# Levels and tokens of the RWKV blocks made for a whole block at a time, and the keyed products moved to earlier slots

## The chip, the cores and the metric

The kernel runs on one core of a Trainium2 chip. The metric is the device time of one execution in microseconds. A core has several engines with an instruction queue each: TensorE (PE: matmul, with its weight loads shown as PEld), VectorE (DVE), ScalarE (ACT), GpSimd (POOL) and SyncE (SP, which issues most DMAs).

## What is computed

The reference is a backbone of two layers over 512 latent and 256 context tokens of width 1024. In each layer one input projection feeds a convolution module and a two-way RWKV-7 recurrence side by side; an output projection and a SwiGLU FFN follow. The part that matters here is the recurrence, over tokens, for 8 heads of 64 and in both directions:

```python
def step(s, inp):
    r_t, k_t, v_t, w_t, kk_t, b_t = inp
    sa = -jnp.einsum("bhvk,bhk->bhv", s, kk_t)
    s = (s * w_t[:, :, None, :] + sa[..., None] * b_t[:, :, None, :]
         + v_t[..., None] * k_t[:, :, None, :])
    y = jnp.einsum("bhvk,bhk->bhv", s, r_t) if emit else None
    return s, y
```

The rest of a layer, cut to what surrounds it:

```python
ux = modulate(rmsnorm(x, norm1_g[l]), sh1, sc1) @ w_in[l]
yc, s_f, s_b = rwkv_scans(prep_c, s_zero, s_zero, emit=not last)
yx, _, _ = rwkv_scans(prep_x, s_f, s_b, emit=True)
mix_x = concatenate([conformer_conv(ux[..., :CONV_IN], *cv), rwkv_out(yx, prep_x, *post)])
x = x + gt1 * (mix_x @ w_out[l])
x = x + gt2 * swiglu(modulate(rmsnorm(x, norm2_g[l]), sh2, sc2), ffn_wg[l], ffn_wu[l], ffn_wd[l])
```

## The kernel before, in words

Per layer there is an input stage, a **mixer stage** and an FFN stage. Dense products (helper `mm`, L234) take their operands as a high and a low part in a fast f32 format (`wh`, `wl`, and `h` or `mid`); the small products of the recurrence are plain f32.

The mixer handles the recurrence in 12 **blocks** b per layer: pair p of heads (b // 3) and group gi of four chunks of 64 tokens (b % 3). Each block goes through these parts, all of them Python generators that yield between steps:

- `prep(b)`: for each direction two products with the low-rank weights `lr` on PE, then a chain of ScalarE and VectorE (tanh, a scan, exponentials, products) that leaves the keys `bk` and the keyed rows `KR`. Its temporaries `tmp` and `tw`, and `bk`, have one buffer each, `KR` has three.
- `z_part(b)`: `grams(b)` makes the keyed products `G` from `KR` and `bk` (two steps, half a block each), then `base(b)` sends their diagonal pieces out by DMA (`d0`), reads them back as `Dt`, inverts 64 pieces of 16x16 at once on VectorE (`XT`) and writes them to `dimg` in DRAM.
- `t_part(b, hf)`: `inverses` loads the small inverses `Tm` from `dimg`, and `levels` joins them to 64x64 inverses in four steps. In each, small products on PE (64x64 or 32x32) are evicted by ScalarE (`W`, `Tm`) or VectorE, and the next step uses them. At the end `KR` is copied into `G`. This is done for half a block (hf) at a time.
- `tokens(b, hf)`: transposes of `bk` into `tT` and of the values into `UV`, in two steps, also for half a block.
- `chain(b, s)`: the serial part, three steps for each of the four chunks.

The order is laid down by `weave`. In every block b all parts that are due (chains of b, levels and tokens of later blocks, prep and z_part of b + 2, convolution steps, the dense input projection cut into pieces) are lanes; a lane with `(first, slots)` and n steps puts step i at the slot first + slots * (i + 1) / n of 16, and the steps are issued in the order of their slots. PE keeps this order as it is written (`manual_schedule`); for the other engines and for SP's queue the framework's scheduler sets it. So an early slot means an early place in PE's queue, and PE waits there for what the step needs. The numbers stand in `PLAN`, per layer; `prologue` does the same for the first blocks of a layer.

Before the change the levels of a block's first half stand at slots 13 to 16 of the block ahead (`t0`), those of its second half at slots 1 to 4 of the block itself (`t1`); tokens are split in the same manner (`tok0`, `tok1`); prep(b + 2) has its steps at 3.3, 4.7 and 6, and z_part(b + 2) its steps at 10.3, 11.7 and 13.

Of the kernel before, what the change touches and what calls it, by code (L numbers as in the profile page):

```python
# [27 lines left out]
C = 64  # L28
# [52 lines left out]
def _pack(i):  # L81
# [45 lines left out]
    for nf in FPARTS:  # L127
# [22 lines left out]
         lanes={"chains": (0, 16), "t1": (0, 4), "t0": (12, 4), "tok1": (0.6, 3.26), "tok0": (13, 2), "prep": (2, 4),  # L150
                "z": (9, 4), "bonus": (3.89, 12.11), "pair_prep": (8, 8), "pair_out": (0, 13)},
         prologue={"pair_prep": (-1.3, 1.2), "prep0": (-0.3, 0.8), "z0": (0.9, 0.58), "tok00": (1.99, 1.08), "tok01": (1.94, 0.38), "prep1": (2.4, 1.0),
                "z1": (3.58, 0.6), "t0": (3.89, 0.86), "tok10": (4.12, 0.2)},
# [4 lines left out]
         lanes={"chains": (0, 16), "t1": (0, 4), "t0": (12.5, 3.5), "tok1": (0, 2.35), "tok0": (13, 2), "prep": (2, 4),  # L158
                "z": (9, 5.03), "bonus": (1.41, 13.65), "pair_prep": (7.33, 7.84), "pair_out": (0, 13)},
         prologue={"pair_prep": (-1.7, 1.2), "prep0": (-0.44, 0.74), "z0": (0.93, 0.52), "tok00": (1.52, 0.47), "tok01": (1.79, 0.39), "prep1": (1.97, 0.98),  # L160
                "z1": (3.6, 0.6), "t0": (3.98, 0.73), "tok10": (4.3, 0.3)},
# [9 lines left out]
def net(ctx: ExitStack, tc: tile.TileContext, I, out):  # L171
# [369 lines left out]
    for l in range(DEPTH):  # L541
# [213 lines left out]
        def prep(b):  # L755
# [42 lines left out]
            BS[b] = dict(KR=KR, bk=bk, vr=vr, pc=pc, emit=emit, G={}, tT={}, UV={}, T={})  # L798
# [35 lines left out]
        def tokens(b, hf):  # L834

            p, gi = divmod(b, 3)
            P, B = PS[p], BS[b]
# [3 lines left out]
            B["tT"][hf] = tT  # L841
            B["UV"][hf] = UV
            pt = [bank(), bank()]
            for s in range(2):
                for d in range(2):
                    cc = 2 * hf + s
                    o = 64 * (2 * s + d)
                    for hh in range(2):
                        hs = slice(64 * hh, 64 * hh + 64)
                        PE.transpose(pt[hh][:, o:o + 64],  # L850
                                     bk[hs, d, cc, hh:hh + 2, :].rearrange("p j t -> p (j t)"), ident[hs, hs])
            for hh in range(2):
                act(tT[:, hh, :, :], pt[hh][:, 0:256].rearrange("p (q j) -> p q j", j=64))
            yield
            pv = bank()
            for s in range(2):
                for d in range(2):
                    cc = 2 * hf + s
                    c0 = C * nat(0, gi, cc)
                    src = B["vr"][:, cc, :] if d else u[f"v{p}"][:, c0:c0 + 64]  # L860
                    o = 128 * (2 * s + d)
                    PE.transpose(pv[0:64, o:o + 128], src, ident)  # L862
            for hh in range(2):
                act(UV[64 * hh:64 * hh + 64, :, hh, :],
                    pv[0:64].rearrange("p (q h j) -> p q h j", q=4, h=2)[:, :, hh, :])
            yield
# [29 lines left out]
        def inverses(b, hf):  # L896

            Tm = s2.tile([128, 4, 2, 64], F32, tag="Tm", name=nm("Tm"), bufs=4)
            for hh in range(2):
                w = 64 - 64 * hh  # L900
                nc.sync.dma_start(out=Tm[w:w + 64].rearrange("p q x c -> p q (x c)"),
                                  in_=dimg[b % 3][8 * hf + 4 * hh:8 * hf + 4 * hh + 4, 0:8192]
                                  .rearrange("q (r c) -> r q c", c=128))
            BS[b]["T"][hf] = Tm

        def levels(b, hf):

            B = BS[b]
            Gt, Tm = B["G"][hf], B["T"][hf]
            lm = lmask.rearrange("p (x t) -> p x t", x=2)  # L910
            pW = bank()
            for q in range(4):
                for hh in range(2):
                    w = slice(64 - 64 * hh, 128 - 64 * hh)
                    mm(pW[w, 64 * q:64 * q + 64], Gt[w, hh, q, 0:64], Tm[w, q, 0, :])
            W = s2.tile([128, 4, 64], F32, tag="W", name=nm("W"))
            act(W.rearrange("p q t -> p (q t)"), pW[:, 0:256])
            yield
            pX = bank()
            for q in range(4):  # L920
                for hh in range(2):
                    w = slice(64 - 64 * hh, 128 - 64 * hh)
                    mm(pX[w, 64 * q:64 * q + 64], W[w, q, :], Tm[w, q, 1, :])
            for q in range(4):
                for hh in range(2):
                    w = slice(64 - 64 * hh, 96 - 64 * hh)
                    mm(pX[w, 256 + 32 * q:288 + 32 * q], Tm[w, q, 1, 0:32], W[w, q, 0:32])
            for hh in range(2):
                w = slice(64 - 64 * hh, 96 - 64 * hh)
                V.copy_predicated(out=Tm[w, :, 0, 0:32], mask=lm[w, 0:1, 0:32].to_broadcast([32, 4, 32]),  # L930
                                  data=pX[w, 256:384].rearrange("p (q t) -> p q t", t=32))
            V.copy_predicated(out=Tm[:, :, 1, :], mask=lm[:, 1:2, :].to_broadcast([128, 4, 64]),
                              data=pX[:, 0:256].rearrange("p (q t) -> p q t", t=64))
            yield
            pW = bank()
            W = s2.tile([128, 4, 64], F32, tag="W", name=nm("W"))
            for q in range(4):
                for hh in range(2):
                    w = 64 - 64 * hh
                    mm(pW[w + 32:w + 64, 32 * q:32 * q + 32], Gt[w:w + 32, hh, q, 32:64], Tm[w:w + 32, q, 0, 0:32])  # L940
            for hh in range(2):
                w = slice(96 - 64 * hh, 128 - 64 * hh)
                act(W[w, :, 0:32], pW[w, 0:128].rearrange("p (q t) -> p q t", t=32))
            yield
            pX = bank()
            for q in range(4):
                for hh in range(2):
                    w = 64 - 64 * hh
                    mm(pX[w:w + 32, 32 * q:32 * q + 32], W[w + 32:w + 64, q, 0:32], Tm[w + 32:w + 64, q, 1, 32:64])
            for hh in range(2):  # L950
                w = slice(64 - 64 * hh, 96 - 64 * hh)
                act(Tm[w, :, 1, 32:64], pX[w, 0:128].rearrange("p (q t) -> p q t", t=32))

            for hh in range(2):
                act(Gt[64 - 64 * hh:128 - 64 * hh, hh, :, 0:64].rearrange("p (s d) t -> p d s t", d=2),
                    B["KR"][64 * hh:64 * hh + 64, :, 2 * hf:2 * hf + 2, 0, :])
            yield

        def chain(b, s):
# [3 lines left out]
            Gt, tT, UV, Tm = (B[k][s // 2] for k in ("G", "tT", "UV", "T"))  # L963
# [8 lines left out]
            for d, hh in DH:  # L972
# [3 lines left out]
                mm(pz[w, 64 * d:64 * d + 64], Gt[k, hh, q, 0:64], UV[k, q, hh, :])  # L976
# [15 lines left out]
            for d, hh in DH:  # L992
                w = slice(64 - 64 * hh, 128 - 64 * hh)
                mm(pu[w, 64 * d:64 * d + 64], Tm[w, 2 * s_ + d, 1, :], Z[w, 64 * d:64 * d + 64])
            pu3 = pu[:, 0:128].rearrange("p (d t) -> p d t", d=2)
            with soon():
                act(UV[64:128, 2 * s_:2 * s_ + 2, 0, :], pu3[64:128], AF.Copy, scale=-1.0)
                ts(UV[0:64, 2 * s_:2 * s_ + 2, 1, :], pu3[0:64], -1.0, 0.0)
            yield

            if not fin:
                pm = bank("c")
                for d, hh in DH:
                    hs = slice(64 * hh, 64 * hh + 64)
                    mm(pm[hs, 64 * d:64 * d + 64], tT[:, hh, 2 * s_ + d, :], UV[:, 2 * s_ + d, hh, :])
                Sn = s2.tile([128, 2, 64], F32, tag="S", name=nm("S"))
                with soon():
# [154 lines left out]
        def t_part(b, hf):  # L1162
            inverses(b, hf)
            yield from levels(b, hf)

        def chains(b):
            for s in range(4):
# [4 lines left out]
        with tc.manual_schedule(engines={mybir.EngineType.PE}):  # L1172
            for name, ps in zip(FIRST, pf):
# [3 lines left out]
            start = {"pair_prep": (pair_prep(0), 3), "prep0": (prep(0), 3), "z0": (z_part(0), 3), "tok00": (tokens(0, 0), 2),  # L1177
                     "tok01": (tokens(0, 1), 2), "prep1": (prep(1), 3), "z1": (z_part(1), 3), "t0": (t_part(0, 0), 4),
                     "tok10": (tokens(1, 0), 2)}
# [6 lines left out]
            for b in range(12):  # L1186
# [9 lines left out]
                lane("t1", t_part(b, 1), 4)  # L1196
# [197 lines left out]
```

## Time and profile before

| | us |
|---|---|
| median of 3 runs | 2250.86 |
| lowest, highest | 2250.03, 2259.32 |
| the profiled execution | 2251.84 |
| its span, first to last instruction | 2250.0 |

| stage (first layer) | window, us | PE idle, us |
|---|---|---|
| mixer, blocks 0 to 11 | 130 to 565 | 26.1 |
| FFN | 690 to 1240 | 3.6 |

A row of the profile's timeline has start and duration in us, engine, line, operation, `out<-in` by the program's tile names, shapes and the count of merged instructions; in brackets the idle time of the engine before it and what ended it. An f32 product is recorded twice, a dense one once. L234 is the helper of all matmuls, L222 that of all ScalarE operations, so groups are told apart by their tiles: `pw<-wl,lr` is prep, `pw<-KR,bk` a gram, `pw<-Tm,G`, `pw<-Tm,W` and `pw<-W,Tm` are levels, L850 and L862 the transposes of tokens, and `pc<-...` the chain. A wait row has waiter, what it waited for, total us, count and longest. Granted clock is the share of TensorE's full clock.

### The profile page before, as it was taken

What the parts mean: (1) busy time and instruction counts of PE and PEld (TensorE: products, weight loads), DVE (VectorE), ACT (ScalarE), POOL (GpSimd) and SP (SyncE); (2) the same over time, 40 slices, a digit from 0 to 9 for tenths busy, and PEclk for the clock granted to TensorE, in tenths of its full rate; (3) what the DMA queues carried; (4) which work ended last, traced back from release to release, by engine and by line L of the source; (5) the groups of instructions that cost most, each with busy time, mean ns of one, the idle gap of its engine ahead of it and who ended that gap; (6) DMA issues with size and microseconds to landing.
All of it is one profiled execution on the core that took longest, in us unless ns stands there. A gap on an engine that the chain in (4) does not pass through costs nothing.

```text
span 2250.0 us, 46614 instructions
## 1 busy us (share of the span) xinstructions
PE 2134.0 (95%) x18800; PEld 1724.2 (77%) x18800; DVE 1333.6 (59%) x3249; ACT 952.3 (42%) x2260; POOL 193.0 (9%) x524
## 2 busy tenths in 40 slices
PE   6999999999999999999999999999999989999996
PEld 4777777777687888888888776767676678888885
DVE  5578887878648332332333766778777755343446
ACT  5455645555325211211212545566656534222223
POOL 0102121312010000000000000121212010000000
PEclk9999999999799999999999999899999999999999
DMA  8233422333554112111122413132424552223223
GB/s 289 65 100 90 108 77 68 84 98 107 146 176 150 57 52 71 61 61 66 51 72 86 139 49 94 37 84 66 114 52 116 169 204 75 95 90 106 86 98 118
DMA packets 196007, 220.72 MB, mean 98 GB/s; under 512 B 110352, under 2 KB 139792, under 8 KB 195792
## 3 DMA queue, kind: packets, MB, share of 16 engines
q1 hardware_dynamic: 194640, 215.65, 31.9%
q8 instruction: 148, 2.42, 0.4%
q10 hardware_dynamic: 1152, 2.10, 0.2%
q14 instruction: 67, 0.55, 0.1%
HBM read 192.49 MB, written 25.21 MB: 97 GB/s over the span
## 4 chain that ended last, share of the span: by engine, by line
PE 77%; ACT 8%; DVE 7%; DMA 3%; POOL 2%; issue 2%; SPq 0%; POOLq 0%; ACTq 0%; DVEq 0%
PE pd L234 38%; PE pw L234 33%; PE pc L234 5%; ACT tmp L222 2%; ACT UV L222 1%; DVE wl L228 1%; DMA raw<-in_wd 1%; DMA Dt<-d 1%; PE pw L862 1%; ACT wh L222 1%; DVE acc L225 1%; PE pw L850 1%; ACT Tm L222 0%; DVE xtmp L228 0%; POOL rq L385 0%
## 5 line engine op out<-in xcount | busy, mean ns | idle before, releaser
L234 PE MATMUL pd<-h,wh 128*128 128x512 f32 (+2 forms) x2496 | 686.5, 364 | 6.6 <-ACT h L222 4.5
L222 ACT ACTIVATE wh<-raw 128x1024 fp32r<-128x1024 f32 (+2 forms) x234 | 220.6, 944 | 714.1 <-PE pw L234 317.2
L234 PEld LDWEIGHTS pd<-h,wh 128*128 128x128 f32 (+1 forms) x2496 | 424.9, 190 | 80.0 <-ACT h L222 5.8
L234 PE MATMUL pd<-h,wl 128*128 128x512 f32 (+2 forms) x1248 | 426.6, 365 | 0.0
L228 DVE TENSOR_TENSOR wl<-raw,wh 128x1024 fp32r<-128x1024 f32 (+2 forms) x234 | 252.6, 1081 | 239.1 <-ACT wh L222 237.6
L234 PE MATMUL pw<-h,wh 128*128 128x512 f32 (+1 forms) x1264 | 316.4, 349 | 1.7 <-DVE x L225 1.7
L234 PEld LDWEIGHTS pd<-h,wl 128*128 128x128 f32 (+1 forms) x1248 | 223.8, 189 | 35.7 <-issue 1.6
L234 PEld LDWEIGHTS pw<-h,wh 128*128 128x128 f32 x1264 | 210.3, 189 | 37.3 <-DVE x L225 1.9
L225 DVE SCALAR_TENSOR_TENSOR acc<-z,cw,acc 128x497 f32<-128x497 f32 (+9 forms) x336 | 209.7, 644 | 2.1 <-ACT acc L222 1.4
L234 PE MATMUL pw<-h,wl 128*128 128x512 f32 (+1 forms) x632 | 193.4, 351 | 0.0
L234 PE MATMUL pd<-mid,wh 128*128 128x512 f32 (+1 forms) x568 | 136.6, 344 | 5.0 <-ACT wh L222 4.9
L228 DVE TENSOR_TENSOR ft<-ft,pw 128x512 f32<-128x512 f32 (+1 forms) x67 | 37.8, 590 | 171.2 <-PE pw L234 170.8
L234 PE MATMUL pw<-mid,wh 128*128 128x512 f32 (+1 forms) x568 | 136.5, 343 | 0.6 <-ACT wh L222 0.6
L234 PEld LDWEIGHTS pw<-h,wl 128*128 128x128 f32 x632 | 106.9, 189 | 15.3
L234 PEld LDWEIGHTS pd<-mid,wh 128*128 128x128 f32 x568 | 93.4, 189 | 20.6 <-ACT wh L222 6.5
L234 PEld LDWEIGHTS pw<-mid,wh 128*128 128x128 f32 x568 | 93.7, 189 | 14.4 <-ACT wh L222 0.8
L970 POOL TENSOR_TENSOR Q<-S,pc 128x128 f32<-128x128 f32 x80 | 44.7, 559 | 537.7 <-DVE S L225 183.5
L234 PE MATMUL pd<-mid,wl 128*128 128x512 f32 (+1 forms) x284 | 87.6, 347 | 2.3 <-DVE wl L228 2.3
L234 PE MATMUL pw<-mid,wl 128*128 128x512 f32 (+1 forms) x284 | 87.4, 346 | 0.6 <-DVE wl L228 0.6
L225 DVE SCALAR_TENSOR_TENSOR x<-pw,mod,x 128x512 f32<-128x512 f32 (+1 forms) x60 | 40.1, 672 | 80.4 <-PE pw L234 80.4
L228 DVE TENSOR_TENSOR xtmp<-XT,Dt 64x15 f32<-64x15 f32 (+4 forms) x360 | 75.3, 209 | 11.5 <-DMA Dt<-d 7.2
L774 POOL MEMSET tmp<- 128x4 f32 x48 | 5.2, 108 | 876.3 <-PE pw L234 632.3
(190 smaller groups left out, 3298.0 us busy)
## 6 DMA issues: line engine op xcount, KB each, us to landing
ada<-in_ada SPq DMA_DIRECT2D x96, 512.0 KB, 4.2
raw<-in_wgu SPq DMA_DIRECT2D x88, 512.0 KB, 3.4
raw<-in_win SPq DMA_DIRECT2D x42, 512.0 KB, 3.4
raw<-in_wd SPq DMA_DIRECT2D x48, 320.0 KB, 2.9
Tm<-dimg SPq DMA_DIRECT2D x96, 128.0 KB, 3.6
raw<-in_wd SPq DMA_DIRECT2D x32, 384.0 KB, 3.0
d<-G SPq DMA_DIRECT2D x96, 64.0 KB, 2.1
raw<-in_wo SPq DMA_DIRECT2D x16, 384.0 KB, 3.2
```

The lines of the kernel that those rows point to most:

```text
L222: A.activation(out=out, in_=in_, func=func, **k)
L225: V.scalar_tensor_tensor(out=out, in0=in0, scalar=scalar, in1=in1, op0=op0, op1=op1, **k)
L228: V.tensor_tensor(out=out, in0=a, in1=b, op=op)
L234: PE.matmul(out=out, lhsT=lhsT, rhs=rhs, start=start, stop=stop)
L774: G.memset(lx[:, :, 0:1], 0.0)
L850: PE.transpose(pt[hh][:, o:o + 64], bk[hs, d, cc, hh:hh + 2, :].rearrange("p j t -> p (j t)"), ident[hs, hs])
L862: PE.transpose(pv[0:64, o:o + 128], src, ident)
L970: G.tensor_tensor(out=Q, in0=S, in1=pc[:, :, s:s + 1].to_broadcast([128, 2, 64]), op=MUL)
```

## The change

Levels and tokens are made for a whole block in the same number of steps as half a block before: each step's products on PE are twice as many and each eviction twice as wide. `tT`, `UV` and `Tm` hold a block, with two buffers instead of four; `W` is twice as wide, with one buffer instead of two. A level's second step uses two PSUM banks where it used one. `weave` also takes a tuple of absolute slots.

The lanes move: levels of block b + 1 to slots 10.67, 12, 13.5 and 14.8; tokens of b + 1 to 0.6 and 1.33; the steps of prep(b + 2) from 3.3, 4.7 and 6 to 2.9, 4.45 and 6.0; those of z_part(b + 2) from 10.3, 11.7 and 13 to 6.57, 8.23 and 9.9.

```diff
-         lanes={"chains": (0, 16), "t1": (0, 4), "t0": (12, 4), "tok1": (0.6, 3.26), "tok0": (13, 2), "prep": (2, 4),
-                "z": (9, 4), "bonus": (3.89, 12.11), "pair_prep": (8, 8), "pair_out": (0, 13)},
+         lanes={"chains": (0, 16), "t": (0, (10.6667, 12.0, 13.5, 14.8)), "tok": (0, (0.6, 1.3333)), "prep": (1.34, 4.67),
+                "z": (4.9, 5), "bonus": (3.89, 12.11), "pair_prep": (8, 8), "pair_out": (0, 13)},
...
-        def tokens(b, hf):
+        def tokens(b):
...
-            tT = s2.tile([128, 2, 4, 64], F32, tag="tT", name=nm("tT"), bufs=4)
-            UV = s2.tile([128, 4, 2, 64], F32, tag="UV", name=nm("UV"), bufs=4)
+            tT = s2.tile([128, 2, 8, 64], F32, tag="tT", name=nm("tT"), bufs=2)
+            UV = s2.tile([128, 8, 2, 64], F32, tag="UV", name=nm("UV"), bufs=2)
...
-            for s in range(2):
+            for cc in range(4):
                 for d in range(2):
...
-        def inverses(b, hf):
-
-            Tm = s2.tile([128, 4, 2, 64], F32, tag="Tm", name=nm("Tm"), bufs=4)
+        def inverses(b):
+
+            Tm = s2.tile([128, 8, 2, 64], F32, tag="Tm", name=nm("Tm"), bufs=2)
...
-            for q in range(4):
+            for q in range(8):
                 for hh in range(2):
                     w = slice(64 - 64 * hh, 128 - 64 * hh)
-                    mm(pW[w, 64 * q:64 * q + 64], Gt[w, hh, q, 0:64], Tm[w, q, 0, :])
-            W = s2.tile([128, 4, 64], F32, tag="W", name=nm("W"))
-            act(W.rearrange("p q t -> p (q t)"), pW[:, 0:256])
+                    mm(pW[w, 64 * q:64 * q + 64], G8(q)[w, hh, 0:64], Tm[w, q, 0, :])
+            W = s2.tile([128, 8, 64], F32, tag="W", name=nm("W"), bufs=1)
+            act(W.rearrange("p q t -> p (q t)"), pW)
             yield
-            pX = bank()
-            for q in range(4):
+            pX, pY = bank(), bank()
+            for q in range(8):
...
+                at = slots if isinstance(slots, tuple) else [first + slots * warp((i + 1) / n) for i in range(n)]
...
-                lane("t1", t_part(b, 1), 4)
...
-                    lane("tok1", tokens(b + 1, 1), 2)
-                    lane("t0", t_part(b + 1, 0), 4)
+                    lane("tok", tokens(b + 1), 2)
+                    lane("t", t_part(b + 1), 4)
...
-                    lane("tok0", tokens(b + 2, 0), 2)
```

The second layer's lanes change in the same way (`z` from (9, 5.03) to (4.9, 5)). In the prologue `t0` and `tok0` are whole blocks, and `tok01` and `tok10` are gone. The other index changes follow from the shapes.

How this moves instructions is shown at three places, as rows of the built programs (`out<-in`, the size of the output, and xN for N equal instructions; tile names end in a running number, which differs between the two programs).

PE, first layer, from the second `lr` pair of the prep of block 9 on. Before:

```order
L234 MATMUL pw_6129<-wl_768,lr_5633 128x256 x2
L234 MATMUL pw_6150<-cst,ev_5786 128x2
L234 MATMUL pc_6156<-UV_5168,G_4953 64x64 x4
L234 MATMUL pd_6078<-h_199,wl_5581 128x512
L234 MATMUL pd_6078<-h_201,wh_5579 128x512
L234 MATMUL pd_6078<-h_202,wh_5579 128x512
L234 MATMUL pd_6078<-h_201,wl_5581 128x512
L234 MATMUL pc_6171<-KR_4770,S_6103 64x64 x4
L234 MATMUL pc_6176<-Z_6161,Tm_5691 64x64 x4
L234 MATMUL pd_6078<-h_203,wh_5579 128x512
```

The same place now, up to the first products of `KR` and `bk`:

```order
L234 MATMUL pw_5961<-wl_768,lr_5544 128x256 x2
L234 MATMUL pw_5984<-cst,ev_5687 128x2
L234 MATMUL pc_5990<-UV_5162,G_4752 64x64 x4
L234 MATMUL pd_5932<-h_199,wl_5461 128x512
L234 MATMUL pd_5932<-h_201,wh_5459 128x512
L234 MATMUL pd_5932<-h_202,wh_5459 128x512
L234 MATMUL pd_5932<-h_201,wl_5461 128x512
L234 MATMUL pw_6006<-KR_5906,bk_5907 128x128
L234 MATMUL pw_6007<-KR_5906,bk_5907 128x128
```

The first gram of the block stands 7 rows below the second `lr` pair now; before it stood 25 rows below. Ahead of that pair stand, in the program of after, the first `lr` pair, five dense products of 512 columns and two groups of the chain.

PE, first layer, the second level step of a block, before (`Tm,W` and `W,Tm` are the step's products, the L850 rows after them are tokens):

```order
L234 MATMUL pd_4327<-h_202,wh_3805 128x256
L234 MATMUL pd_4327<-h_201,wl_3807 128x256
L234 MATMUL pw_4536<-Tm_4459,W_4471 64x64 x8
L234 MATMUL pw_4536<-W_4471,Tm_4459 32x32 x8
L850 MATMUL pw_4558<-cst,bk_4197 128x64
```

and now:

```order
L234 MATMUL pc_4944<-UV_4038,tT_4037 64x64 x4
L234 MATMUL pc_4900<-G_3633,UV_4038 64x64 x4
L234 MATMUL pw_4960<-Tm_4912,W_4934 64x64 x16
L234 MATMUL pw_4961<-W_4934,Tm_4912 32x32 x16
L234 MATMUL pd_4596<-h_207,wl_4240 128x256
```

Two groups of 8 became one of 16; the second group of 8 stood elsewhere before.

DVE, first layer, the first direction of the prep of block 7, from the scan (L779) on. Before:

```order
L779 SCALAR_TENSOR_TENSOR tmp_4776<-one_95,tmp_4776 128x260
L228 TENSOR_TENSOR XT_4474<-XT_4474,xtmp_4475 64x13x3
L225 SCALAR_TENSOR_TENSOR S_4810<-pc_4805,pc_3538,Q_4684 128x64
L228 TENSOR_TENSOR xtmp_4475<-XT_4474,Dt_4473 64x28
L225 SCALAR_TENSOR_TENSOR S_4810<-pc_4805,pc_3538,Q_4684 128x64
L228 TENSOR_TENSOR XT_4474<-XT_4474,xtmp_4475 64x14x2
L228 TENSOR_TENSOR KR_4770<-kk_3796,tmp_4776 128x4x64
L228 TENSOR_TENSOR xtmp_4475<-XT_4474,Dt_4473 64x15
L228 TENSOR_TENSOR KR_4770<-r_3293,tmp_4776 128x4x64
L228 TENSOR_TENSOR XT_4474<-XT_4474,xtmp_4475 64x15
```

and now:

```order
L779 SCALAR_TENSOR_TENSOR tmp_4670<-one_95,tmp_4670 128x260
L225 SCALAR_TENSOR_TENSOR S_4697<-pc_4692,pc_3472,Q_4624 128x64 x2
L228 TENSOR_TENSOR y_3457<-y_3457,pc_4650 128x64
L228 TENSOR_TENSOR KR_4664<-kk_3767,tmp_4670 128x4x64
L228 TENSOR_TENSOR KR_4664<-r_3294,tmp_4670 128x4x64
L228 TENSOR_TENSOR y_3457<-y_3457,pc_4650 128x64
L231 TENSOR_SCALAR mod_1629<-pw_4731,prm 128x2
L228 TENSOR_TENSOR tmp_4670<-tmp_4670,k_2849 128x4x64
L225 SCALAR_TENSOR_TENSOR tw_4671<-tw_4671,kk_3767 128x256
L228 TENSOR_TENSOR bk_4665<-tmp_4670 128x4x64
```

The steps of the small inverses (`XT`) no longer stand between those of the prep chain; they stand ahead of its scan.

More of the change, by code (lines that the diff above doesn't have):

```diff
@@ L852, in tokens @@
             for hh in range(2):
-                act(tT[:, hh, :, :], pt[hh][:, 0:256].rearrange("p (q j) -> p q j", j=64))
+                act(tT[:, hh, :, :], pt[hh].rearrange("p (q j) -> p q j", j=64))
             yield
[L855 to L865, printed above, removed]
+            for hf in range(2):
+                pv = bank()
+                for s in range(2):
+                    for d in range(2):
+                        cc = 2 * hf + s
+                        c0 = C * nat(0, gi, cc)
+                        src = B["vr"][:, cc, :] if d else u[f"v{p}"][:, c0:c0 + 64]
+                        o = 128 * (2 * s + d)
+                        PE.transpose(pv[0:64, o:o + 128], src, ident)
+                for hh in range(2):
+                    act(UV[64 * hh:64 * hh + 64, 4 * hf:4 * hf + 4, hh, :],
+                        pv[0:64].rearrange("p (q h j) -> p q h j", q=4, h=2)[:, :, hh, :])
             yield
@@ L951, in levels @@
                 w = slice(64 - 64 * hh, 96 - 64 * hh)
[L952 to L956, printed above, removed]
+                act(Tm[w, :, 1, 32:64], pX[w, 0:256].rearrange("p (q t) -> p q t", t=32))
+            for hf in range(2):
+                for hh in range(2):
+                    act(B["G"][hf][64 - 64 * hh:128 - 64 * hh, hh, :, 0:64].rearrange("p (s d) t -> p d s t", d=2),
+                        B["KR"][64 * hh:64 * hh + 64, :, 2 * hf:2 * hf + 2, 0, :])
             yield
@@ L962, in chain @@
             KR, pc, emit = B["KR"], B["pc"], B["emit"]
-            Gt, tT, UV, Tm = (B[k][s // 2] for k in ("G", "tT", "UV", "T"))
+            Gt, tT, UV, Tm = B["G"][s // 2], B["tT"], B["UV"], B["T"]
             s_ = s % 2
@@ L1144, in weave @@
         def weave(*lanes):
-            order = sorted((first + slots * (warp((i + 1) / n) if warp else (i + 1) / n), j)
-                           for j, (first, slots, n, _, *w) in enumerate(lanes) for warp in [w[0] if w else None] for i in range(n))
-            for _, j in order:
+            order = []
+            for j, (first, slots, n, _, *w) in enumerate(lanes):
+                warp = w[0] if w else lambda q: q
+                at = slots if isinstance(slots, tuple) else [first + slots * warp((i + 1) / n) for i in range(n)]
+                order += [(at[i], j) for i in range(n)]
+            for _, j in sorted(order):
                 next(lanes[j][3], None)
@@ L1160, in z_part, with t_part @@
             yield
-        def t_part(b, hf):
-            inverses(b, hf)
-            yield from levels(b, hf)
+        def t_part(b):
+            inverses(b)
+            yield from levels(b)
         def chains(b):
@@ L1176, in net @@
             B8 = 24 * T / PCOL
[L1177 to L1179 removed]
+            start = {"pair_prep": (pair_prep(0), 3), "prep0": (prep(0), 3), "z0": (z_part(0), 3), "tok0": (tokens(0), 2), "prep1": (prep(1), 3), "z1": (z_part(1), 3), "t0": (t_part(0), 4)}
             weave(*((e[0] + d * B8, w * B8, *reversed(start[n])) for n, (d, w) in plan["prologue"].items()), (0, e[-1], e[-1], proj))
```

80 lines of the change are left out of this document (40 added, 40 removed).

## The prediction

> **What bounds the kernel now.** I read the page's engine table and its chain first, then the windows by stage, then the list of what TensorE waits for.
>
> ```profile
> PE 2134.0 (95%) x18800; PEld 1724.2 (77%) x18800; DVE 1333.6 (59%) x3249; ACT 952.3 (42%) x2260; POOL 193.0 (9%) x524
> ...
> PE 77%; ACT 8%; DVE 7%; DMA 3%; POOL 2%; issue 2%; SPq 0%; POOLq 0%; ACTq 0%; DVEq 0%
> ```
>
> ```profile
> 130.00:565.00 435.00, 408.92 (x5559) 321.33 (x5557) 362.36 (x1074) 249.31 (x722) 88.48 (x202) 0.97 0.35 91
> 690.00:1240.00 550.00, 546.44 (x3179) 471.41 (x3178) 198.42 (x320) 128.92 (x192) 0.00 (x0) 1.00 0.21 68
> 1310.00:1765.00 455.00, 432.81 (x5198) 320.28 (x5200) 330.35 (x978) 274.78 (x781) 74.83 (x224) 0.97 0.31 82
> ```
>
> TensorE is the bound: 95% busy and 77% of the chain. The window rows give length, then busy time of PE, weight loads, DVE, ACT and POOL, then the granted clock. The change touches only the two mixer stages (first and third window row). There PE is idle for 26.1 and 22.2 us, at a mean clock of 0.97; DVE, at 362 of 435 us, is the next engine. PE runs its instructions in the written order, so a step that stands too early stops everything behind it.
>
> ```profile
> PE pw L234 <- POOL gsq L386: 7.6, 6, 2.2
> PE pw L234 <- DVE bk L225: 5.1, 8, 1.3
> ...
> PE pw L850 <- ACT Tm L222: 4.4, 5, 1.3
> ...
> PE pw L234 <- ACT bk L222: 2.4, 4, 1.1
> ```
>
> These rows name who PE waited for, the total, the count and the longest. The two with bk matter: keyed products (grams) waited 12 times, 7.5 us in all, for the tile bk that the decay step (prep) of the same block makes. The present distance between prep and grams is thus just about used up.
>
> **Part 1: fewer, larger groups on PE.** No matmul is added or removed. Six interruptions of the dense stream go in each of 24 blocks: four level steps and two token steps.
>
> ```profile
> 338.12 0.40 PE L234 MATMUL pd<-h,wh 128*128 128x256 f32 x2
> 338.36 0.28 PE L234 MATMUL pd<-h,wl 128*128 128x256 f32 x1
> 338.57 0.68 PE L234 MATMUL pw<-Tm,W 64*64 64x64 f32 x16
> 339.18 0.44 PE L234 MATMUL pw<-W,Tm 32*32 32x32 f32 x16
> 339.55 0.47 PE L850 MATMUL pw<-cst,bk 64*128 64x64 f32 x8
> ```
>
> The columns are start, duration, instruction and count (an f32 product counts twice). Two dense products take 0.24 us (338.12 to 338.36), the one ahead of the small group 0.21 instead of 0.12: 0.09 us for going in. The eight 64x64 products take 0.61 us to the next group, although within such a group they start 0.058 us apart, which would be 0.46; about 0.1 to 0.15 us is paid inside and coming out. So an interruption costs about 0.2 us, and 6 x 24 x 0.2 = 28.8, **28 us saved**. Where a group has neighbours of its own shape less is saved: at 0.1 us each it is 14 us; at 0.25 us, 36. ScalarE and VectorE issue fewer, longer evictions; neither sets the end, so I take nothing for that.
>
> **Part 2: the grams move up to the prep step.** Before, prep puts its two decay products (lr) at slots 3.3 and 4.7 (first layer) and the first gram stands at 10.3. Now they stand at 2.9, 4.45 and 6.57. What has to happen in between is a chain of ScalarE and VectorE, once per direction, and the second direction cannot begin before the first has left the single buffers tmp and tw. Its shortest case in the trace is the first prep of the second layer:
>
> ```profile
> 1319.91 1.02 PE L234 MATMUL pw<-wl,lr 128*128 128x256 f32 x4
> ...
> 1320.97 0.47 ACT L222 ACTIVATE tmp<-pw,der 128x256 f32<-128x256 f32 x1 [1.25 <-PE pw L234]
> ...
> 1325.79 0.41 ACT L222 ACTIVATE bk<-bk 64x256 f32<-64x256 f32 x1 [0.21 <-DVE bk L228]
> ...
> 1326.23 0.47 ACT L222 ACTIVATE tmp<-pw,der 128x256 f32<-128x256 f32 x1
> ...
> 1330.67 0.41 DVE L225 SCALAR_TENSOR_TENSOR bk<-tw,tmp 128x256 f32<-128x256 f32 x1
> ...
> 1331.17 0.42 ACT L222 ACTIVATE bk<-bk 64x256 f32<-64x256 f32 x1
> ...
> 1331.95 1.11 PE L234 MATMUL pw<-KR,bk 64*128 64x64 f32 x16
> ```
>
> One direction takes 5.2 us (1320.97 to 1326.20), the second 5.4, and both with the products ahead 11.7 us from 1319.91 to 1331.59. In an ordinary block it is longer, since other VectorE work stands between:
>
> ```profile
> 191.80 1.13 PE L234 MATMUL pw<-wl,lr 128*128 128x256 f32 x4
> ...
> 195.65 1.03 PE L234 MATMUL pw<-wl,lr 128*128 128x256 f32 x4
> ...
> 206.29 0.94 PE L234 MATMUL pw<-KR,bk 64*128 64x128 f32 x12
> ```
>
> Here the gram starts 14.5 us after the first lr. The changed order of VectorE has little between the steps of a direction (see the rows of the change), so I take 12.0 us, near the short case; 11 and 13.5 are the ends.
>
> Against that stands PE's own work between the first lr and the first gram. In the block whose rows are shown it is now two lr pairs, some nine dense products and four small groups:
>
> ```profile
> 313.63 1.13 PE L234 MATMUL pw<-wl,lr 128*128 128x256 f32 x4
> 314.41 0.59 PE L234 MATMUL pd<-h,wh 128*128 128x256 f32 x2
> ...
> 316.07 0.45 PE L234 MATMUL pc<-UV,tT 128*64 128x64 f32 x8
> 316.36 0.40 PE L234 MATMUL pc<-G,UV 128*64 128x64 f32 x8
> 316.69 0.44 PE L234 MATMUL pw<-Tm,W 32*32 32x32 f32 x16
> ```
>
> An lr pair takes 0.78 us to the next row, a chain group 0.29 to 0.33, a dense product of 512 columns 0.23 (1314.20 to 1314.43 in the rows further down): 2 x 0.78 + 9 x 0.23 + 4 x 0.33 = 5.0, with the changes of shape some 5.5 us. Counted in the same way over all the blocks that are prepared two blocks ahead (10 in each layer), it lies between 4.9 and 7.2, mean 5.9 us. So PE stops for 12.0 - 5.9 = 6.1 us, 20 times: **122 us added**, from 20 x 5.1 = 102 to 20 x 7.6 = 152. The wait is PE's own; behind it stand the chain's products and the dense stream, so nothing else can fill it. The 7.5 us of old bk waits go (**-8**).
>
> **Part 3: the clock after a stop.**
>
> ```profile
> 1303.00:1307.00 4.00, 0.02 (x1) 0.00 (x0) 3.23 (x7) 3.51 (x6) 0.46 (x3) 1.00 0.62 197
> 1307.00:1314.00 7.00, 6.96 (x23) 5.99 (x24) 3.21 (x6) 0.91 (x2) 3.09 (x14) 0.52 0.00 0
> ...
> 358.00:365.00 7.00, 6.83 (x50) 4.75 (x50) 2.85 (x8) 4.43 (x14) 0.53 (x3) 0.52 0.22 37
> ...
> 1396.00:1403.00 7.00, 6.90 (x47) 4.90 (x49) 4.29 (x8) 1.01 (x3) 0.11 (x1) 0.51 0.06 13
> ...
> 1437.00:1451.00 14.00, 14.00 (x138) 11.81 (x138) 7.26 (x17) 3.84 (x12) 0.89 (x4) 0.51 0.30 64
> ```
>
> ```profile
> 1313.04 0.63 PE L234 MATMUL pd<-h,wl 128*128 128x512 f32 x1
> ...
> 1314.20 0.39 PE L234 MATMUL pd<-h,wl 128*128 128x512 f32 x1
> 1314.43 0.63 PE L234 MATMUL pd<-h,wh 128*128 128x512 f32 x2
> ```
>
> PE stopped for 4 us, and the next 7 us ran at a granted clock of 0.52: a dense product started 0.42 us after the last (1313.04 to 1313.46), afterwards 0.23. Seven such microseconds lose 7 x 0.48 = 3.4 us. Part of a low stretch will lie in the stop itself, so I take two thirds, 2.2 us, for each of 20 stops: **44 us added** (28 at 1.4, 68 at 3.4). The dips from 1396 and 1437 stand at old gram waits and go: 21 x 0.49, **-10**.
>
> [...]
>
> **Part 4: the rest.** Levels now stand at slots 10.7 to 14.8 and tokens at 0.6 and 1.3 of the next block; each level step keeps over one slot to the next, as before. The token transposes no longer follow a level's eviction closely, so the 4.4 us at L850 go; and each stop lets VectorE and ScalarE catch up, which I put at half of the 15 us that the POOL gsq row and the other small waits of its kind hold: **-12** together, between 0 and -30. The four Tm loads of a block are now issued together on SP's queue. No row has PE waiting for Tm by DMA, and a load lands in 3.6 us (page) with its source written a block earlier: nothing. W has a single buffer; its next writer stands two steps, about 3 slots, later: nothing.
>
> **The sum**, against the profiled execution of 2251.84 us (within 1 us of the median, 2250.86): 2251.8 + 122 + 44 - 8 - 10 - 28 - 12 = **2360 us**, 4.8% slower.
>
> **Rivals.**
> - *The clock costs little*, because the low stretches end within the stops: the 44 go, and the 10 stay gained: 2316. Against it: the half rate at 1307 and 358 came after the stop, not in it. Chance 0.14.
> - *The clock stays low longer*, as from 1437 (14 us): 3 us more a stop, 2420. Chance 0.08.
> - *The stops are given back*: they only take the place of the 48 us that PE is idle in the mixers anyway. With 102 added, no clock loss, and 48, 10 and 36 gained it is 2260. Each old wait would have to be due to a late VectorE or ScalarE; the gsq row (POOL) and the data loads speak against it. Chance 0.04.
> - *Faster*: the chain from lr to bk is mostly queueing behind other VectorE work, and without that it shrinks to PE's 5.9 us. It decides at the point where stop and clock cost less than the gain of 58: a stop of (58 / 20) or 2.9 us, so 8.8 us from the first lr to bk. At 7 us it would be 2251.8 + 22 - 58 = 2216. Against it: the short case has almost nothing between its steps and still takes 11.7. Chance 0.03.
>
> **How the numbers follow.** The forecast, stops with half the clock behind them, holds 0.71: its ends are 2310 and 2400. The range is to leave out no more than 2 in 10; 2290 to 2415 takes in most of the case without clock loss and the start of the longer one. Within 0.5% (2241 to 2263, about what a measurement of this kernel can tell from no change) lies the third rival, 0.04; faster 0.03; slower 0.93.
>
> **What would show it.** Right: PE waits for bk (ScalarE or VectorE) some 20 times with 4 to 8 us each; the mean clock in both mixer windows falls under 0.9; the first gram starts 11 to 13.5 us after the first lr; small groups stand in fewer, larger rows; outside the mixers nothing moves. Wrong: bk ready in under 9 us; or PE's idle time in the mixers still near 50 us.

## The result and the profile after

The changed kernel takes **2358.24 us** (median of 4 runs, 2348.44 to 2359.8), beside 2250.45 us of the kernel before in the same comparison: a ratio of 1.046 with a 95% interval of 1.042 to 1.050. It is 108 us slower. The forecast was 2360 us, and the time lies in its range. The span of the profiled execution went from 2250.0 to 2346.7 us; that execution is the fastest of the four, so the trace holds 97 of the 108 us.

The page of after, its busy time and its chain:

```profile
PE 2138.5 (91%) x18800; PEld 1741.0 (74%) x18800; DVE 1338.5 (57%) x3177; ACT 931.2 (40%) x2092; POOL 200.5 (9%) x524
...
PE 76%; DVE 11%; ACT 7%; DMA 2%; POOL 2%; issue 2%; SPq 0%; POOLq 0%; DVEq 0%; ACTq 0%
```

PE is busy for 4.5 us longer than before (2134.0), so of the 96.7 us that the span grew by 92 are idle time of PE. That the busy time hardly changed does not mean that the clock cost nothing: a gain and a loss lie in it, which experiment 2 takes apart. In the chain the share of VectorE rose from 7% to 11%: time in which PE stood and something on VectorE decided. Two engines have fewer instructions, as the change says: 3177 on VectorE for 3249, 2092 on ScalarE for 2260.

The windows of after by stage (columns as before; behind the granted clock stand the DMA share and GB/s), then two short windows in block 4 of the first layer:

```profile
125.00:605.00 480.00, 413.48 (x5538) 330.58 (x5538) 372.08 (x1048) 240.52 (x645) 90.31 (x203) 0.92 0.31 83
730.00:1280.00 550.00, 546.43 (x3223) 477.62 (x3224) 205.30 (x329) 132.74 (x197) 0.00 (x0) 1.00 0.22 71
1345.00:1850.00 505.00, 436.28 (x5093) 326.87 (x5093) 321.80 (x920) 258.46 (x687) 77.34 (x221) 0.89 0.28 72
240.00:250.60 10.60, 7.69 (x79) 5.34 (x77) 6.73 (x18) 7.84 (x24) 0.94 (x4) 1.00 0.67 198
250.60:257.40 6.80, 4.72 (x34) 4.00 (x34) 3.41 (x9) 1.24 (x4) 0.11 (x1) 0.50 0.10 21
```

The stretch between the mixers (second row) is what it was: idle for 3.6 us in 550, full clock. In the mixers PE is idle for 66.5 and 68.7 us, where it was 26.1 and 22.2 in windows with about as many matmuls, and the clock fell from 0.97 to 0.92 and 0.89. The last two rows show one block: full rate, then 6.8 us at half rate.

What PE waited for in after (total, count, longest):

```profile
PE pw L234 <- DVE bk L225: 102.1, 33, 5.4
...
PE pw L234 <- DVE Tm L933: 6.0, 13, 1.0
...
PE pw L861 <- ACT tT L222: 4.8, 7, 1.1
```

One wait holds nearly all of it: keyed products (grams) for the tile bk, 102.1 us where it was 5.1 (and 2.4 by ScalarE). The timeline of the same block 4, from the first decay products (lr) on (of the grams the weight loads, which lead their products):

```profile
240.71 1.13 PE L234 MATMUL pw<-wl,lr 128*128 128x256 f32 x4
...
241.88 0.47 ACT L222 ACTIVATE tmp<-pw,der 128x256 f32<-128x256 f32 x1
...
247.04 0.41 ACT L222 ACTIVATE bk<-bk 64x256 f32<-64x256 f32 x1 [0.88 <-DVE bk L228]
...
247.39 0.41 PEld L234 LDWEIGHTS pw<-KR,bk 64*128 64x128 f32 x4 [0.22 <-DVE bk L225]
...
247.81 0.47 ACT L222 ACTIVATE tmp<-pw,der 128x256 f32<-128x256 f32 x1
...
252.20 0.42 DVE L225 SCALAR_TENSOR_TENSOR bk<-tw,tmp 128x256 f32<-128x256 f32 x1
...
252.67 1.46 PEld L234 LDWEIGHTS pw<-KR,bk 64*128 64x128 f32 x12 [4.88 <-DVE bk L225]
```

The first direction of the decay step is made from 241.88 to 247.45. PE arrives just then and runs the first two gram products, which are of that direction (four rows, since an f32 product is recorded twice); the next two need the second direction. That one starts at 247.81, when the first has left `tmp`, and its bk is there at 252.6. PE's weight loads stand for 4.9 us (from 247.79), its products for 4.7; the low clock sets in at 250.6, inside the stop, and lasts until 257.4, 4.7 us past its end. So a stop can have two pieces. Of the 33 waits 20 are long, 3.5 to 5.4 us each and 90.3 us together, and they stop the grams of a block in the middle; 11 short ones, 0.2 to 1.7 us, stand ahead of a block's first grams, and 2 more lie in the prologue.

### The profile page after: what moved, and what is told of

Its sections match the earlier page's. It is cut to its first block, busy times and chain, and to the rows that moved or that the text cites. A ratio compares the mean times of both kernels' runs of the same rounds, so it can differ in the third digit from the quotient of the medians.

```text
span 2346.7 us, 46268 instructions
## 1 busy us (share of the span) xinstructions
PE 2138.5 (91%) x18800; PEld 1741.0 (74%) x18800; DVE 1338.5 (57%) x3177; ACT 931.2 (40%) x2092; POOL 200.5 (9%) x524
## 4 chain that ended last, share of the span: by engine, by line
PE 76%; DVE 11%; ACT 7%; DMA 2%; POOL 2%; issue 2%; SPq 0%; POOLq 0%; DVEq 0%; ACTq 0%
PE pd L234 38%; PE pw L234 32%; PE pc L234 6%; ACT tmp L222 2%; DVE acc L225 1%; DVE tmp L779 1%; DVE wl L228 1%; ACT UV L222 1%; DVE xtmp L228 1%; ACT wh L222 1%; DVE XT L228 1%; PE pw L861 1%; DMA ada<-in_ada 1%; DVE tmp L228 1%; DMA raw<-in_wd 1%
## 5 line engine op out<-in xcount | busy, mean ns | idle before, releaser
L234 PE MATMUL pd<-h,wh 128*128 128x512 f32 (+2 forms) x2496 | 694.0, 367 | 6.6 <-ACT h L222 4.5
L234 PEld LDWEIGHTS pd<-h,wh 128*128 128x128 f32 (+1 forms) x2496 | 429.9, 192 | 79.9 <-ACT h L222 5.9
L234 PE MATMUL pw<-KR,bk 64*128 64x128 f32 (+1 forms) x768 | 86.5, 342 | 104.2 <-DVE bk L225 102.1
L234 PEld LDWEIGHTS pw<-KR,bk 64*128 64x128 f32 x768 | 69.4, 232 | 125.6 <-DVE bk L225 111.5
L972 POOL TENSOR_TENSOR Q<-S,pc 128x128 f32<-128x128 f32 x80 | 51.8, 647 | 525.6 <-DVE S L225 318.4
```

What stands on the lines that cost most here:

```text
L234: PE.matmul(out=out, lhsT=lhsT, rhs=rhs, start=start, stop=stop)
L972: G.tensor_tensor(out=Q, in0=S, in1=pc[:, :, s:s + 1].to_broadcast([128, 2, 64]), op=MUL)
```

## The experiments

The theory was the prediction's: early grams stop PE, and the stop costs clock as well. The rivals were that the new places of levels and tokens, or the shape of the groups, cost the time, or that the clock costs little. The edits are to the changed kernel, except for the second, which is to the kernel before. Ratios are to the kernel before, with 95% intervals.

### 1. The grams at their old slots

```diff
-                "z": (4.9, 5), ...
+                "z": (9, 4), ...      (second layer: (9, 5.03))
```

> The changed kernel with one thing undone: the keyed products and small inverses stand again at slots 10.3 to 13 (first layer; 10.7 to 14 in the second). Levels and tokens stay whole blocks. Theory A (the time went into TensorE stopping for bk, 20 times, and into the halved clock behind the stops): the waits for bk fall from 102 us to under 12, the clock returns to about 0.97, and the time is that of before less the saved interruptions: 2205 to 2230 us, a ratio to before of 0.98 to 0.99. Theory B (the whole-block groups cost it themselves, by wider evictions or by levels that come late): the time stays above 2300 us, and waits at the levels and the transposes of tokens hold most of it.

Measured: 2280.02 us (2274.64 to 2285.56), ratio 1.013 [1.011, 1.015]. This one edit takes back 78 of the 108 us, and the waits for bk are gone, but it stays 30 us above before, and so 50 us above what was expected. Waits, and two places of the timeline in the second layer:

```profile
PE pw L234 <- DMA Tm<-dimg: 25.2, 15, 7.0
...
PE pw L234 <- DVE bk L225: 4.2, 5, 2.0
```

```profile
1440.46 0.47 PE L234 MATMUL pw<-Tm,G 64*64 64x64 f32 x2 [7.01 <-DMA Tm<-dimg]
...
1799.61 0.47 PE L234 MATMUL pw<-Tm,G 64*64 64x64 f32 x2 [6.78 <-DMA Tm<-dimg]
```

A new wait took the old one's place: the first level step waits for the load of the small inverses. All 15 of these waits lie in the second layer. There the last step of z now ends at slot 14.03, and the levels start at 10.67 of the next block, 12.6 slots later; the small inverses (VectorE's `XT` steps, then a way through memory) have to be made in between. The expectation had left this out. So the early place of the grams had a purpose in the changed program: it made room for the earlier levels.

### 2. Only the grams and the decay step moved

```diff
# the kernel before
-    "prep": (2, 4), "z": (9, 4), ...
+    "prep": (1.34, 4.67), "z": (4.9, 5), ...      (both layers)
```

> The kernel before with one thing done: prep and keyed products at the new slots (2.9, 4.45, 6.0 and 6.57, 8.23, 9.9). Levels and tokens stay half blocks. TensorE's own work from the first decay product to the first keyed product is 6.9 us on the mean here (5.9 in the changed kernel). Theory A: 20 stops of about 12.4 - 6.9 = 5.5 us, 110 us, and some 40 us by the clock, less some 15 us of old waits: 2365 to 2400 us, slower than the changed kernel by the interruptions. Theory B: within 0.5% of before, about 2250 us.

Measured: 2387.0 us (2384.5 to 2393.81), ratio 1.061 [1.059, 1.063], as expected. What PE waited for, and the busy time on its page:

```profile
PE pw L234 <- DVE bk L225: 91.3, 30, 6.1
```

```profile
PE 2179.6 (91%) x18800; PEld 1755.7 (74%) x18800; DVE 1345.3 (56%) x3249; ACT 961.4 (40%) x2260; POOL 196.5 (8%) x524
```

The move alone costs 137 us. It is the whole loss, and more: the rest of the change (levels and tokens for a whole block, their new slots) gives 2387.0 - 2358.2 = 29 us back.

The traces show the parts. The products and their groups are those of the kernel before, and yet PE is busy for 2179.6 us here, 46 us more than before (2134.0), at a mean granted clock of 0.948 (before 0.975): read as the clock's part, since nothing else in these products differs but their order. PE's idle time grew by 90 us, from 116.0 to 206.1. The changed kernel, at a clock of 0.950, is idle for about as long (208.2 us) but busy for 41 us less (2138.5): there the larger groups show.

### 3. The stop filled with work

```diff
                 pg = [bank(), bank()]
+                if hf == 0 and b >= 2:
+                    for _ in range(20):
+                        mm(pg[0], h[0][0].bitcast(F32R)[:, 0:128], h[0][0].bitcast(F32R)[:, 0:512])
```

The added products go into the bank that the grams overwrite.

> The changed kernel with 20 dense products of 512 columns added ahead of the first keyed product of each block from the third on (20 x 0.23 = 4.6 us, so inside the stop); their result goes to the bank that the keyed products then overwrite. They keep TensorE busy while it waits. If the halved clock behind the stops costs time (theory A, 44 us in the prediction): the low stretches of the clock become few, and the time falls by 25 to 45 us, to 2313 to 2333, although TensorE does more. Rival (the low clock lies beside other waits and costs nothing): no change or up to 20 us more, 2358 to 2378.

Measured: 2322.39 us (2320.55 to 2339.87), ratio 1.034 [1.030, 1.037], as expected: **36 us faster than after, though PE does 400 products more**. Two rows of the timeline of the same block 4, the windows beside them, and the wait for bk:

```profile
243.04 4.83 PE L234 MATMUL pw<-h 128*128 128x512 f32 x20
247.80 1.59 PE L234 MATMUL pw<-KR,bk 64*128 64x128 f32 x16
```

```profile
243.00:247.80 4.80, 4.80 (x26) 3.68 (x21) 2.53 (x7) 2.90 (x9) 0.11 (x1) 1.00 0.28 109
247.80:258.00 10.20, 10.14 (x127) 7.66 (x128) 6.02 (x16) 4.49 (x10) 0.51 (x2) 1.00 0.07 14
```

```profile
PE pw L234 <- DVE bk L225: 20.3, 19, 3.2
```

Here the 20 products fill the stop, the grams come 11.4 us after the first lr (236.38) and the clock stays at 1.00, where after had 0.50. The mean clock is 0.975 again, as in before. The added products take about 96 us (20 x 4.8), and the waits for bk fell by 82 us (102.1 to 20.3); so some 14 us of the products are time that the stops had not cost already, and the clock's part of the loss lies between 36 and, by this estimate, 50 us.

### 4. The grams half way

```diff
-                "z": (4.9, 5), ...
+                "z": (7, 4), ...      (both layers)
```

> The changed kernel with the keyed products and small inverses at slots 8.33, 9.67 and 11 in both layers. TensorE's own work from the first decay product to the first keyed product is then 9.7 us on the mean, against some 12.4 until bk is there. Theory A: 20 stops of about 2.7 us, 54 us, with 15 to 35 us by the clock, so 2280 to 2310 us. Rival (any place that close behind prep delays VectorE and ScalarE as a whole, not by the distance): near the changed kernel, over 2335 us, or with no loss at all, under 2235.

Measured: 2323.52 us (2314.5 to 2336.38), ratio 1.033 [1.029, 1.037], 14 us above what was expected.

```profile
PE pw L234 <- DVE bk L225: 55.1, 22, 6.2
```

With the first gram at slot 8.33 instead of 6.57 the waits for bk halve, the load of the inverses is hardly waited for (0.4 us, once), and a third of the loss goes. The waits came out as expected (55.1 us for 54); the clock did not. It stays at 0.955 on the mean, where the changed kernel has 0.950, and PE is busy for 2151.6 us, 13 more than there (and 43 more than in experiment 8, which has the same groups and few stops). So stops of about half the length cost no less of the clock here, and the expected 15 to 35 us were too few.

### 5. Whole blocks in the old order

```diff
-   "t": (0, (10.6667, 12.0, 13.5, 14.8)), "prep": (1.34, 4.67), "z": (4.9, 5), ...
+   "t": (12, 4), "prep": (2, 4), "z": (9, 4), ...      (second layer: (12.5, 3.5), (2, 4), (9, 5.03))
```

> After the first undoing left a new wait (TensorE waited 25 us for the load of the small inverses, since the levels stood 2.3 slots nearer to them): the changed kernel with levels, prep, keyed products and small inverses at the slots of before (levels 13 to 16, or 13.4 to 16 in the second layer; prep 3.3 to 6; keyed products from 10.3 or 10.7). Levels and tokens stay whole blocks, tokens at 0.6 and 1.33. If the grouping itself saves 28 us (theory A, part 1 of the prediction): waits for the load of Tm under 5 us, and 2205 to 2235 us, a ratio of 0.98 to 0.993. If the grouping gives back what it saves (theory B: wider evictions, waits at the transposes of tokens): 2245 to 2275 us.

Measured: 2262.32 us (2241.4 to 2268.84, 10 runs), ratio 1.003 [1.000, 1.006]. By the ratio that is 7 us more than before, by the medians 12; seven of the ten runs took 2260 to 2269 us and three 2241 to 2249, and the trace is of one of the seven. The first theory, that grouping is worth its 28 us wherever it stands, fell; the second, that it is given back, held. Waits, and one place of the timeline:

```profile
PE pw L234 <- DVE Tm L933: 12.9, 22, 1.4
...
PE pw L861 <- ACT Tm L222: 7.5, 7, 1.8
```

```profile
253.41 0.69 PE L234 MATMUL pw<-W,Tm 32*32 32x32 f32 x32
...
254.45 0.72 DVE L929 COPY_PREDICATED Tm<-lmask,pw 128x512 f32<-128x512 uint8 x1
...
256.84 0.44 DVE L933 COPY_PREDICATED Tm<-lmask,pw 32x256 f32<-32x256 uint8 x1
...
257.33 0.24 PE L234 MATMUL pw<-Tm,G 32*32 32x32 f32 x2 [1.26 <-DVE Tm L933]
257.53 0.43 DVE L933 COPY_PREDICATED Tm<-lmask,pw 32x256 f32<-32x256 uint8 x1
...
258.02 0.69 PE L234 MATMUL pw<-Tm,G 32*32 32x32 f32 x30 [0.44 <-DVE Tm L933]
```

The third level step needs the two copies of L933, and these stand behind the large one of L929 and behind steps of the small inverses and other work on VectorE: 3.9 us from the products to the second copy. In the kernel before the copies are half as wide, and the two small ones stand ahead of the large one. Groups of its costliest instructions, of before and then of after:

```profile
L930 DVE COPY_PREDICATED Tm<-lmask,pw 32x128 f32<-32x128 uint8 x96 | 28.2, 293 | 31.7 <-PE pw L234 29.6
L932 DVE COPY_PREDICATED Tm<-lmask,pw 128x256 f32<-128x256 uint8 x48 | 20.5, 427 | 0.0
```

```profile
L933 DVE COPY_PREDICATED Tm<-lmask,pw 32x256 f32<-32x256 uint8 x48 | 20.9, 435 | 1.5
L929 DVE COPY_PREDICATED Tm<-lmask,pw 128x512 f32<-128x512 uint8 x24 | 17.5, 730 | 12.1 <-PE pw L234 9.3 <-DMA raw<-in_win 2.9
```

By these means the third step could go on after 2 x 0.29 = 0.59 us of copies before; now it is 0.73 + 2 x 0.435 = 1.60 us.

### 6 and 7. Slots between the old and the new

```diff
# 6: everything about a slot later
+   "t": (0, (11.9, 13.2, 14.5, 15.8)), "tok": (0, (0.6, 2.2)), "prep": (0, (2.5, 3.9, 6.0)), "z": (0, (9.7, 10.7, 11.6)), ...
# 7: levels and tokens as in the change, grams late enough for bk
+   "prep": (0, (2.5, 3.9, 6.0)), "z": (0, (9.3, 10.3, 11.0)), ...
```

> The changed kernel with places worked out from the two distances that the runs show: from the first decay product to the first keyed product 13 us of TensorE's own work (it needs some 12.4), and from the small inverses to the levels 16.3 slots (15.7 made no wait, 13.7 did). Prep at 2.5, 3.9 and 6.0, keyed products at 9.7 and 10.7, small inverses at 11.6, levels of the next block at 11.9, 13.2, 14.5 and 15.8, tokens at 0.6 and 2.2 so that the second step follows the eviction less closely. Theory A: no wait above some 10 us for bk and for the load of Tm, and 2205 to 2230 us, faster than both kernels. Theory B: 2240 us or more.

Measured for 6: 2286.46 us (2279.67 to 2297.56), ratio 1.018 [1.013, 1.022]; the first theory missed by 56 us or more, and the second (2240 us or more) held. One premise of the expectation does not fit the record: 13.7 slots from the small inverses to the levels is the distance in the first layer of experiment 1, and all waits for the load were in the second, at 12.6.

```profile
PE pc L234 <- ACT UV L222: 30.0, 31, 2.8
PE pw L234 <- DVE Tm L933: 19.1, 25, 2.4
```

The waits for bk are small (4.3 us), but the chain's wait for `UV` is 30.0 us, where the kernel before has 8.2 in 15 waits, and the copies of the levels cost 19.1. The reading that the chain lost the cover of other products is argued from the list, not shown.

> The changed kernel with levels and tokens at its own slots (levels 10.67, 12, 13.5 and 14.8, tokens 0.6 and 1.33), prep at 2.5, 3.9 and 6.0, keyed products at 9.3 and 10.3 and small inverses at 11. TensorE's own work from the first decay product to the first keyed product is 12.1 us on the mean. The last two runs lost 13 and 19 us at the third level step, which waits for VectorE's copies of the second, where the steps stood 1.0 and 1.3 slots apart, and one lost 30 us at the chain. If the level steps' distance is what counts, the level waits fall to about 6 us as in the changed kernel, and the time is 2215 to 2245 us. If the early slots of a block are short of other work for TensorE (levels have left slots 0 to 4 and prep stands earlier), the chain's waits for UV stay near 30 us and the time is 2255 to 2290 us.

Measured for 7: 2257.55 us (2248.16 to 2275.13, 10 runs), ratio 1.001 [0.998, 1.004]: no difference from the kernel before. Neither theory held whole: the waits of the levels fell as the first said, but the time is in the range of the second, whose sign, 30 us of waits for `UV`, is not there.

```profile
PE pw L234 <- POOL kk L386: 13.4, 7, 3.5
PE pw L234 <- DVE bk L225: 11.0, 10, 2.5
PE pc L234 <- ACT UV L222: 10.5, 12, 3.2
...
PE pw L234 <- DVE Tm L933: 2.2, 5, 0.9
```

With levels and tokens as in the change, moving the grams and the lr products takes out 101 us of the 108. The changed slots of the levels do their work (L933 falls from 12.9 us in experiment 5 to 2.2), but PE still waits for bk, for `kk` and for `UV`.

### 8 and 9. The copies in the old order, then the grams later once more

```diff
# 8 = 7, and the large copy (L929) behind the two small ones (L933)
# 9 = 8, and
-   "z": (0, (9.3, 10.3, 11.0)), ...
+   "z": (0, (9.75, 10.7, 11.4)), ...
```

> The same as the run ahead of it, with the order of VectorE's copies after the second level step as it was before the change: the two quarter copies, for which the third step waits, ahead of the large one (0.7 us). If the third step waits for them because they stand behind the large one: its waits for VectorE fall from their value in the run ahead to under 2 us, and the time falls by 3 to 12 us. Rival (VectorE is late as a whole): no difference above 3 us.

> The kernel of e8_halves_first with the keyed products at slots 9.75, 10.7 and 11.4 instead of 9.3, 10.3 and 11.0. In e8 the keyed products still waited 11.7 us for bk in 10 waits (longest 2.5), in the kernel with these products at 9.7 it was 4.3 us in 7. Theory (A), the remaining distance from the decay products costs what the list says: these waits fall under 6 us, the levels and their loads keep 15 slots of distance and wait no more than in e8, and the time is 4 to 10 us below that of e8, so 2243 to 2250, ratio 0.995 to 0.999. Theory (B), what PE waits for is set by what VectorE and ScalarE can do in a block, so that a wait removed here stands a few instructions later at another tile (the level's copies or UV): the time stays at 2250 to 2262, ratio 0.999 to 1.004.

Measured: 8 takes 2253.47 us (2240.0 to 2257.39, 10 runs), ratio 0.999 [0.997, 1.002]; 9 takes 2254.53 us (2244.48 to 2258.84, 12 runs), ratio 1.001 [0.999, 1.003]. Neither can be told from the kernel before, nor 8 from 7: the third step's waits for the copies, 2.2 us in 7, are gone, but the 4 us that the median fell by are within the noise. The busy time and the waits of 8, then the waits of 9:

```profile
PE 2108.9 (94%) x18800; PEld 1719.8 (77%) x18800; DVE 1330.4 (59%) x3177; ACT 935.7 (42%) x2092; POOL 211.0 (9%) x524
```

```profile
PE pw L234 <- DVE bk L225: 11.7, 10, 2.5
PE pc L234 <- ACT UV L222: 11.2, 14, 3.2
...
PE pw L234 <- DMA Tm<-dimg: 3.1, 3, 2.5
```

```profile
PE pc L234 <- ACT UV L222: 19.3, 25, 2.1
...
PE pw L234 <- DMA Tm<-dimg: 7.3, 8, 2.4
...
PE pw L234 <- DVE bk L225: 3.3, 6, 1.2
```

In 8 PE is busy for 25 us less than in the kernel before (2108.9 against 2134.0): the fewer, larger groups do save PE time, near what part 1 says (in 7 it is 18 us less, in 9 it is 14). Most of it comes out as idle time. The traced execution of 8 is, at 2242.56 us, 11 us faster than the median; even there 16 of the 25 us are lost in idle time (131.9 us, before 116.0), and in that of 9, at 2251.14 us, 13 of the 14. Experiment 9 shows where a wait goes: bk went from 11.7 to 3.3 us, and `UV` and the inverses' load took up 12.3 between them. The second theory of its expectation held: a wait removed here stands a few instructions later at another tile. A way that was not tried is a second buffer of `tmp` and `tw`, so that the second direction of the decay step need not wait until the first has left them, as it does in block 4 of after (247.81); whether there is room for it was not shown. Whether a shorter chain from lr to bk would bring the 25 us out stays open.

## Why the prediction was right

By its own steps:

- **Part 2, the stop: right in place and mechanism, too long in the sum by 13 to 24 us.** Twenty stops of 6.1 us less 8 of old waits made 114. The waits for bk rose from 7.5 to 102.1 us, by 95; PE's idle time rose by 90 in the trace of experiment 2; by the medians it is 137 (experiment 2) less 36 or more for the clock (experiment 3), 101 or less. The 20 long waits have a mean of 4.5 us, and 5.1 with the short ones. In block 4 the chain took 11.96 us from lr to the grams of the second direction (12.0 were taken), but PE filled 11.96 - 4.88 - 0.22 = 6.9 us of it rather than 5.9: the first two grams and two short waits of the chain's products for `UV` (0.36 and 0.30) are among it. That the grams can start with the first direction was not foreseen; so of the measures, "the first gram starts 11 to 13.5 us after the first lr" holds for the second direction alone (the first came after 6.7), and of "some 20 times with 4 to 8 us each" the number is right and the length at the lower end.
- **Part 3, the clock: right in kind, and rather too small.** 44 less 10 made 34; filling the stops brought 36, or up to 50 by the estimate there, and the busy time of experiment 2 shows 46. The stretch in block 4 is 6.8 us, near the 7 that were taken, and two thirds of it (4.7 us) lie behind the stop, as taken. Of the measure "under 0.9 in both mixers" one half held (0.89, and 0.92). Of the two dips that were to go for 10 us, only that of 1396 stands at a gram wait in the kernel before (1.27 us for bk, up to 1395.93); the longer one, from 1437, follows waits for `UV` (rows in the last section).
- **Parts 1 and 4, larger groups and the rest: 40 taken, 29 measured** by the medians of experiment 2 and the changed kernel (39 between their profiled executions). That is inside the bounds given (14 to 66), but it holds only there. The sentence that failed is the one on the longer evictions, "neither sets the end, so I take nothing for that". With the grams at a place where PE hardly stops for them, the kernel with larger groups differed from the one before by +12 us (experiment 5), +4 (7) and 0 (8), the last two within the noise: in 5 the next step waits 12.9 us for the doubled copies (L933), in 7 and 8 the waits for `kk`, bk and `UV` grow (13.4, 11.0 and 10.5 us in 7, and 10.7, 11.7 and 11.2 in 8, for 4.8, 5.1 and 8.2 before). In the changed kernel such waits are small, 6.0 us at L933 and 4.8 at the tokens' second step (L861), and the stops give VectorE and ScalarE time to run ahead; that the stops are the reason is argued, not shown.
- **The loads.** "No row has PE waiting for Tm by DMA": in the changed kernel it is 0.6 us in two waits, next to nothing. Experiment 1 shows how thin this is: with z back at 9 PE waits 25.2 us for the same load.
- **The rivals.** "The clock costs little" gave 2316; experiment 3, which takes the clock's part away and adds some 14 us of products, is at 2322, so this rival had the rest of the sum about right and the clock wrong. "The stops are given back" needed PE's idle time in the mixers to stay near 50 us; it is 66.5 + 68.7 = 135. "Faster" needed a chain of under 9 us from lr to bk; in block 4 it was 12.

The prediction had +114 for the stops, +34 for the clock and -40 for the rest, which is 108. The medians give +101, +36 and -29; these add up to 108 by the way they are taken (the first is 137 less the second), so that they do is no proof. The traces of before, experiment 2 and after give +90, +46 and -39 for the 97 us between their profiled executions. The mechanism was right by both counts. That the total is within 2 us was luck: by the medians an excess of 13 in the stops cancels against 2 and 11 that the clock and the rest fell short by.

## What to carry to other kernels

On an engine that runs in the written order, a step that is moved up must be set against the latest of its inputs, counted through the single buffers on the way; here the distance that the old order kept was just about enough (7.5 us of waits for bk in the whole kernel), and the new one made 102.1 us of them. A saving in an engine's busy time need not be a saving in time: the 14 to 25 us of PE in experiments 7 to 9 left the time where it was (ratios of 0.999 to 1.001). Longer evictions that come with larger groups are one place to look: in experiment 5 the third level step waited 12.9 us for the doubled copies, and with the copies that it reads put first the 2.2 us that experiment 7 still had are gone. And when a wait is tuned away, look at which tile it appears next before the slot is moved again: from experiment 8 to 9 the waits for bk fell by 8.4 us, and those for `UV` and the inverses' load grew by 12.3.

## What the runs showed of the hardware

The low clock came behind shorter waits as well. In experiment 5 it was 0.50 from 453.0 to 456.4 and 0.64 on the mean up to 459.8, with PE busy all the time, behind two waits of 1.19 and 1.72 us (two rows of its timeline, then three windows):

```profile
448.73 1.04 PE L234 MATMUL pw<-KR,bk 64*128 64x128 f32 x12 [1.19 <-DVE bk L225]
...
451.80 0.44 PE L234 MATMUL pw<-cst,ev 128*128 128x2 f32 x2 [1.72 <-DVE G L228]
```

```profile
443.00:453.00 10.00, 7.09 (x86) 5.26 (x84) 9.28 (x24) 4.13 (x14) 0.83 (x2) 0.95 0.45 107
453.00:456.40 3.40, 3.40 (x22) 2.65 (x20) 2.49 (x6) 0.87 (x2) 0.00 (x0) 0.50 0.19 39
456.40:459.80 3.40, 3.40 (x35) 3.06 (x32) 2.66 (x6) 0.96 (x4) 0.40 (x1) 0.64 0.09 19
```

If the clock stood at either 0.50 or 1.00 in these windows, the low stretch is some 7 us long: 0.05 x 10 / 0.5 + 3.4 + 0.36 x 3.4 / 0.5 = 6.8 us, an estimate from their three means.

In the kernel before, the stretch from 1437 to 1451, which the prediction shows at 0.51 with PE busy all the time, comes behind two waits of 0.80 and 0.67 us (rows of its timeline):

```profile
1434.74 0.33 PE L234 MATMUL pc<-UV,G 128*64 128x64 f32 x2 [0.80 <-ACT UV L222]
1435.74 0.45 PE L234 MATMUL pc<-UV,G 128*64 128x64 f32 x6 [0.67 <-ACT UV L222]
```

For the new order the prediction counted a loss of clock behind the long stops alone. The stretch from 1437 to 1451 gave away about 14 x 0.49 = 6.9 us (an estimate from its window), while the two waits ahead of it sum to 1.47 us. That such short waits brought the low clock on is read from the order of events alone; no experiment took them out by themselves, and how much it costs in experiments 5 to 9 was not measured by itself.
